# Loading the kept pieces of h for the second ConvGLU phase through SyncE's queue instead of GpSimd's

## The chip, the core and the metric

The kernel runs on one core of a Trainium2 chip. The metric is the device time of one execution, in microseconds (us). Times are given for three runs of the kernel before, and one further execution was taken with the profiler.

The engines are called as the profile calls them: PE is TensorE, DVE is VectorE, ACT is ScalarE, POOL is GpSimd, SP is SyncE. Each works through its own list of instructions in order, and a DMA is an instruction in the list of the engine that issues it.

## What is computed

The reference is a decoder trunk of two layers. After the attention part, each layer does this (cut to what matters):

```python
h = h + mix
h = h + conv_glu(rmsnorm(h, ffn_norm[i]), ffn_w_in[i], ffn_conv_w[i], ffn_conv_b[i], ffn_w_out[i])
...
def conv_glu(hn, w_in, conv_w, conv_b, w_out):
    u, gate_in = jnp.split(hn @ w_in, 2, axis=-1)
    c = (conv_w[0] * shift_right(gate_in, 2) + conv_w[1] * shift_right(gate_in, 1)
         + conv_w[2] * gate_in + conv_b)
    return (jax.nn.gelu(c, approximate=False) * u) @ w_out
```

h is 1024 positions by 1024 features, the middle of the gated part 2816 wide, all in float32. The change lies in the last line: the product with `w_out`, and the residual h that is added to it.

## The kernel before

Float32 products are made of three matmuls: weights and data are each split into a rounded high half (a cast on ACT, line 202) and the rest, the low half (a subtraction on DVE or POOL, line 203); `mm3` multiplies high by high, high by low and low by high (line 228).

Both products of the ConvGLU use Strassen's scheme in Winograd's form: seven block products in place of eight, on sums of blocks. The first phase (`ffn_in`) makes the gated values, adds them up to the seven operands, and writes these to DRAM as the tiles `md` (seven products by eleven pieces of 128x512). It also needs the room that h took, so h has been written to DRAM earlier (`hs`, line 564).

The second phase, `ffn_out`, is run once per layer. It goes through its seven products in order (`jobs`, n = 0 to 6). Each has eleven pieces; a piece is a load of `md` into a `wraw` tile (line 763, three buffers, issued by SP), its two halves `mh` (ACT) and `ml` (DVE), the two halves `whi` (ACT) and `wlo` of a weight block `a`, and twelve matmuls (four output tiles by three). For n = 0 and 1 the low weight half is made on POOL, from n = 2 on DVE. The weight blocks of n = 3 to 6 are sums of the loaded ones, which POOL makes in place (line 742, 44 additions of 128x512 per layer); `a10` is wanted by product 3, `a00` by 4, `a11` by 2 and then, changed, by 5, `a01` by 6.

The output tiles are added on DVE (`add`, line 734) into a new h. Where a quarter of h is first complete but for the residual, `kept` loads the old piece of h from `hs` into a tile `kept` of three buffers and adds it: 16 pieces a layer, four after product 3 (for q = 0 to 3 in the low half of the positions), four after product 4 and eight after product 5. The load is issued by POOL.

A scheduler sets the order of the instructions on each engine from estimated times; a load stands where its buffer is expected to come free. So the first three `kept` loads stand early, and the fourth stands behind the first addition of a kept piece, whose buffer it takes over.

Of the kernel before, what the change touches and what calls it, by code (L numbers as in the profile page):

```python
# [122 lines left out]
class Trunk:  # L123
# [596 lines left out]
    def ffn_out(self, ctx, h, hs, layer, md, first):  # L720


        nc, tc, t = self.nc, self.tc, self.t
        wp, pm = self.wp, self.pm
        Q, N = KD // 2, NFT // 2
        lo, hi = slice(0, BW), slice(BW, S)
        kp = Lines(ctx.enter_context(tc.tile_pool(reuse_waits="tile", name="kept", bufs=3)))
        ap = Lines(ctx.enter_context(tc.tile_pool(reuse_waits="tile", name="wout", bufs=1)))

        a = [[[None] * 2 for m in range(2)] for i in range(N)]  # L730
        late = [(1, 0, i) for i in range(N)]
        for m, k, i in late[:5] + [(m, k, i) for m, k in ((0, 0), (0, 1), (1, 1)) for i in range(N)] + late[5:]:
            a[i][m][k] = ap.tile([P, Q, P], F32, name=f"a{m}{k}_{i}")
        add = lambda out, x, y: nc.vector.tensor_tensor(out=out, in0=x, in1=y, op=OP.add)

        def load(m, k, i):
            nc.sync.dma_start(out=a[i][m][k], in_=t["ffn_w_out"][layer, i, k, m])

        def sums(out, one, two, op):
            def at(i):  # L740
                out_, x, y = [a[i][m][k] for m, k in (out, one, two)]
                nc.gpsimd.tensor_tensor(out=out_, in0=x, in1=y, op=op)  # L742
                return out_
            return at


        plain = lambda m, k: lambda i: a[i][m][k]
        jobs = [(plain(0, 0), (0, 1)), (plain(0, 1), (1, 1)), (plain(1, 1), (1, 0)), (sums((1, 0), (1, 0), (1, 1), OP.add), None),
                (sums((0, 0), (1, 0), (0, 0), OP.subtract), None), (sums((1, 1), (1, 1), (0, 0), OP.subtract), None),
                (sums((0, 1), (0, 1), (0, 0), OP.subtract), None)]  # L750
        for i in list(range(len(first), N)) + list(range(len(first))):
            load(0, 0, i)

        def kept(f, bs):
            x = kp.tile([P, BW], F32, name="kept")
            nc.gpsimd.dma_start(out=x, in_=hs[:, f, bs])
            add(h[:, f, bs], h[:, f, bs], x)

        for n, (weight, ahead) in enumerate(jobs):
            ps = [pm.tile([P, BW], F32, name="mm") for q in range(Q)]  # L760
            for i in range(N):
                raw = wp.tile([P, BW], F32, name="wraw", bufs=self.wbufs[0])
                nc.sync.dma_start(out=raw, in_=md[n][i])
                if ahead:
                    load(*ahead, i)
                xh, xl = [self.block_tile(j, R) for j in range(2)]
                self.split(xh, xl, raw, eng=nc.vector)
                if n == 0 and i < len(first):
                    wh, wl = first[i]
                else:  # L770
                    wh, wl = [wp.tile([P, Q, P], R, name="w" + x, bufs=self.wbufs[1]) for x in ("hi", "lo")]
                    self.split(wh, wl, weight(i), eng=nc.vector if n > 1 else nc.gpsimd)
                for q in range(Q):
                    self.mm3(ps[q], [((wh[:, q], wl[:, q]), (xh, xl))], first=i == 0, last=i == N - 1)
            for q in range(Q):
                h00, h01, h10, h11 = [h[:, 2 * q + m, bs] for m in range(2) for bs in (lo, hi)]
                if n == 0:
                    nc.scalar.copy(out=h01, in_=ps[q])
                elif n == 1:
                    add(h00, ps[q], h01)  # L780
                elif n == 2:
                    nc.scalar.copy(out=h10, in_=ps[q])
                elif n == 3:
                    nc.scalar.copy(out=h11, in_=ps[q])
                    kept(2 * q, lo)
                elif n == 4:
                    add(h01, ps[q], h01)
                    add(h10, h10, h01)
                    add(h11, h11, h01)
                    nc.vector.tensor_copy(out=h01, in_=h11)  # L790
                    kept(2 * q, hi)
                elif n == 5:
                    add(h10, ps[q], h10)
                    add(h11, ps[q], h11)
                    kept(2 * q + 1, lo)
                    kept(2 * q + 1, hi)
                else:
                    add(h01, ps[q], h01)
# [1230 lines left out]
```

## Time and profile before

| | us |
|---|---|
| median of three runs | 3007.69 |
| lowest and highest | 3003.44, 3019.6 |
| the profiled execution | 3006.23 |
| its span in the trace | 3004.5 |

| engine | busy us | share of the span |
|---|---|---|
| PE | 2835.7 | 94% |
| DVE | 2193.2 | 73% |
| ACT | 1341.1 | 45% |
| POOL | 1036.9 | 35% |

The busy times say how much of the span an engine had an instruction running; matmuls are pipelined, and their listed durations overlap, so the distance between two starts is the better measure of a matmul. `ffn_out` runs from about 1229 to 1450 us in layer 0 and from about 2620 to 2845 us in layer 1.

### The profile page before, as it was taken

How to read it: one execution, taken by the hardware profiler on the slowest of the kernel's cores; microseconds unless marked ns; L12 is line 12 of the kernel's file. 1: busy time of each engine (PE TensorE's matmuls, PEld its weight loads, DVE VectorE, ACT ScalarE, POOL GpSimd, SP SyncE). 2: the span in 40 equal slices, each digit the busy share in tenths (PEclk: the TensorE clock that was granted, in tenths of full speed). 3: DMA queues.
4: the chain of work that ended last, by engine and by line, in shares of the span. 5: the costliest groups of instructions: out<-in, count | busy, mean ns of one | idle time of the engine just before them, and what ended most of it. 6: DMA issues, size and time to landing. Idle time of an engine off the chain costs nothing. (4 is left out here: it accounts for less than half of the span.)

```text
span 3004.5 us, 40784 instructions
## 1 busy us (share of the span) xinstructions
PE 2835.7 (94%) x14278; PEld 2191.3 (73%) x14278; DVE 2193.2 (73%) x3290; ACT 1341.1 (45%) x2433; POOL 1036.9 (35%) x800
## 2 busy tenths in 40 slices
PE   8999999999899999969998899999979999996997
PEld 6776777677678888858886656566858888885886
DVE  7766657875798777566798577777489777864787
ACT  6424436663334333424644444344343333443474
POOL 4332420104434444480333500010435444384133
PEclk9999989999999999989999899999989999998998
DMA  4344565535123333733321300012113333363421
GB/s 142 111 147 127 158 199 151 156 96 172 42 99 109 106 105 106 244 97 112 102 90 58 111 18 24 12 43 102 68 51 128 105 106 103 122 234 92 123 64 57
DMA packets 238846, 322.26 MB, mean 107 GB/s; under 512 B 64465, under 2 KB 109009, under 8 KB 238641
## 3 DMA queue, kind: packets, MB, share of 16 engines
q1 hardware_dynamic: 230896, 300.79, 32.1%
q10 hardware_dynamic: 5184, 10.49, 0.9%
q0 software_dynamic: 2560, 8.39, 0.9%
q8 instruction: 112, 1.84, 0.3%
q14 instruction: 94, 0.76, 0.1%
HBM read 219.37 MB, written 99.09 MB: 106 GB/s over the span
## 5 line engine op out<-in xcount | busy, mean ns | idle before, releaser
L228 PE MATMUL mm<-x,whi 128*128 128x512 f32 x1760 | 556.0, 396 | 27.1 <-DVE x L203 14.5
L228 PE MATMUL mm<-mh,wlo 128*128 128x512 f32 x968 | 380.2, 393 | 51.9 <-DVE wlo L203 51.9
L228 PEld LDWEIGHTS mm<-x,whi 128*128 128x128 f32 x1760 | 335.2, 191 | 108.5 <-DVE x L203 22.0
L228 PE MATMUL mm<-xh,whi 128*128 128x512 f32 (+1 forms) x1016 | 405.1, 399 | 6.5 <-ACT xh L208 6.5
L228 PE MATMUL mm<-xh,wlo 128*128 128x512 f32 (+1 forms) x1016 | 397.5, 391 | 1.2 <-POOL wlo L203 1.2
L228 PE MATMUL mm<-xl,whi 128*128 128x512 f32 (+1 forms) x1016 | 390.8, 392 | 0.5 <-DVE xl L209 0.5
L228 PE MATMUL mm<-ml,whi 128*128 128x512 f32 x968 | 380.2, 393 | 1.6 <-DVE ml L203 1.4
L228 PE MATMUL mm<-mh,whi 128*128 128x512 f32 x968 | 379.8, 392 | 0.0
L203 POOL TENSOR_TENSOR wlo<-wraw,whi 128x512 fp32r<-128x512 f32 (+2 forms) x150 | 206.8, 1384 | 429.1 <-ACT whi L202 360.2
L228 PE MATMUL mm<-x,wlo 128*128 128x512 f32 x880 | 345.9, 395 | 1.1 <-DVE wlo L203 1.1
L202 ACT CAST whi<-raw 128x512 fp32r<-128x512 f32 x274 | 169.3, 619 | 323.1 <-PE mm L228 267.0
L203 POOL TENSOR_TENSOR wlo<-raw,whi 128x512 fp32r<-128x512 f32 x114 | 169.6, 1489 | 333.9 <-ACT whi L202 323.5
L228 PEld LDWEIGHTS mm<-mh,wlo 128*128 128x128 f32 x968 | 183.3, 189 | 91.6 <-DVE wlo L203 53.2
L228 PEld LDWEIGHTS mm<-xh,whi 128*128 128x128 f32 x1016 | 195.1, 192 | 50.4 <-ACT xh L208 7.2
L228 PEld LDWEIGHTS mm<-xl,whi 128*128 128x128 f32 x1016 | 194.8, 192 | 44.3 <-issue 5.1
L228 PEld LDWEIGHTS mm<-xh,wlo 128*128 128x128 f32 x1016 | 194.9, 192 | 42.2 <-POOL wlo L203 2.0
L228 PEld LDWEIGHTS mm<-ml,whi 128*128 128x128 f32 x968 | 183.2, 189 | 42.4 <-DVE ml L203 3.1
L228 PEld LDWEIGHTS mm<-mh,whi 128*128 128x128 f32 x968 | 183.6, 190 | 38.8 <-ACT mh L202 0.6
L228 PEld LDWEIGHTS mm<-x,wlo 128*128 128x128 f32 x880 | 168.5, 192 | 37.1 <-DVE wlo L203 2.6
L203 DVE TENSOR_TENSOR ml<-wraw,mh 128x512 fp32r<-128x512 f32 x154 | 134.0, 874 | 65.8 <-ACT mh L202 62.5
L1123 ACT ACTIVATE w<-s 128x512 f32<-128x512 f32 (+1 forms) x192 | 94.0, 491 | 167.1 <-PE s L1121 149.3
L202 ACT CAST whi<-a 128x512 fp32r<-128x512 f32 x148 | 91.9, 622 | 147.6 <-PE mm L228 90.3
(432 smaller groups left out, 5757.0 us busy)
## 6 DMA issues: line engine op xcount, KB each, us to landing
raw<-in_ffn_w_in SPq DMA_DIRECT2D x176, 256.0 KB
md<-u SPq DMA_DIRECT2D x154, 256.0 KB
wraw<-md SPq DMA_DIRECT2D x154, 256.0 KB
a<-in_ffn_w_out SPq DMA_DIRECT2D x88, 256.0 KB
wraw<-in_hyb_w_in SPq DMA_DIRECT2D x52, 256.0 KB
hs<-h SPq DMA_DIRECT2D x32, 256.0 KB
kept<-hs POOLq DMA_DIRECT2D x32, 256.0 KB, 3.0
wraw<-in_ple_w_gate SPq DMA_DIRECT2D x32, 256.0 KB
```

Source lines behind the costliest of these rows:

```text
L202: nc.scalar.copy(out=hi, in_=src)
L203: (eng or nc.gpsimd).tensor_tensor(out=lo, in0=src, in1=hi, op=OP.subtract)
L228: nc.tensor.matmul(ps, lhsT=w, rhs=x, start=first and i == 0, stop=last and i == len(seq) - 1)
L1123: nc.scalar.activation(out=w[:, :n], in_=s[:, :n], func=AF.Exp, scale=MLA_SCALE)
```

## The change

One line of `kept` names another engine:

```diff
         def kept(f, bs):
             x = kp.tile([P, BW], F32, name="kept")
-            nc.gpsimd.dma_start(out=x, in_=hs[:, f, bs])
+            nc.sync.dma_start(out=x, in_=hs[:, f, bs])
             add(h[:, f, bs], h[:, f, bs], x)
```

The 32 loads leave POOL's list and stand in SP's, and the scheduler places them anew. PE's list is the same in both kernels. In the rows below a name ends in the number of its buffer; layer 1 has the same pattern with other numbers.

POOL's list of the kernel before, layer 0, the last additions of weight blocks with the loads of the fourth to seventh kept piece among them:

```order
L742 TENSOR_TENSOR a01_10_11695<-a01_10_11695,a00_10_11684 128x512
L742 TENSOR_TENSOR a11_4_11700<-a11_4_11700,a00_4_11678 128x512
L742 TENSOR_TENSOR a11_5_11701<-a11_5_11701,a00_5_11679 128x512
L756 DMA kept_12765<-hs0_7126 128x512
L742 TENSOR_TENSOR a11_6_11702<-a11_6_11702,a00_6_11680 128x512
L756 DMA kept_13029<-hs0_7126 128x512
L756 DMA kept_13036<-hs0_7126 128x512
L742 TENSOR_TENSOR a11_7_11703<-a11_7_11703,a00_7_11681 128x512
L756 DMA kept_13043<-hs0_7126 128x512
L742 TENSOR_TENSOR a11_8_11704<-a11_8_11704,a00_8_11682 128x512
L742 TENSOR_TENSOR a11_9_11705<-a11_9_11705,a00_9_11683 128x512
L742 TENSOR_TENSOR a11_10_11706<-a11_10_11706,a00_10_11684 128x512
```

In the changed kernel the additions stand there alone; 39 of the 44 additions of a layer stand ahead of the fourth load before, and none stands ahead of it on SP's list.

SP's list of the changed kernel, layer 0, from the last pieces of product 2 (`md0_2`) to the first of product 3:

```order
L763 DMA wraw_12445<-md0_2_9_7825 128x512
L763 DMA wraw_12468<-md0_2_10_7826 128x512
L756 DMA kept_12765<-hs0_7126 128x512
L763 DMA wraw_12499<-md0_3_0_7827 128x512
L756 DMA kept_13029<-hs0_7126 128x512
L756 DMA kept_13036<-hs0_7126 128x512
L763 DMA wraw_12522<-md0_3_1_7828 128x512
L756 DMA kept_13043<-hs0_7126 128x512
L763 DMA wraw_12545<-md0_3_2_7829 128x512
```

Before, the `md` loads stood there one after the other; now the fourth kept load goes out between the last load of product 2 and the first of product 3. On DVE the order of this stretch is unchanged:

```order
L734 TENSOR_TENSOR h2_0_11659<-h2_0_11659,kept_12753 128x512
L203 TENSOR_TENSOR wlo_12384<-a11_6_11702,whi_12383 128x512
L203 TENSOR_TENSOR ml_12426<-wraw_12422,mh_12425 128x512
L734 TENSOR_TENSOR h2_2_11660<-h2_2_11660,kept_12757 128x512
L734 TENSOR_TENSOR h2_4_11661<-h2_4_11661,kept_12761 128x512
L203 TENSOR_TENSOR wlo_12407<-a11_7_11703,whi_12406 128x512
L203 TENSOR_TENSOR ml_12449<-wraw_12445,mh_12448 128x512
L734 TENSOR_TENSOR h2_6_11662<-h2_6_11662,kept_12765 128x512
L203 TENSOR_TENSOR wlo_12430<-a11_8_11704,whi_12429 128x512
L203 TENSOR_TENSOR ml_12472<-wraw_12468,mh_12471 128x512
L203 TENSOR_TENSOR wlo_12453<-a11_9_11705,whi_12452 128x512
L203 TENSOR_TENSOR ml_12502<-wraw_12499,mh_12501 128x512
```

The scheduler moves the four additions of kept pieces that belong behind product 3 up into product 2; nothing of this moved with the change. `kept_12765` is the fourth piece, and the low halves of the ninth, tenth and eleventh weight block of product 2 stand behind its addition.

SP's list of the changed kernel, layer 0, at the end of product 5 (`md0_5`):

```order
L763 DMA wraw_13218<-md0_5_7_7856 128x512
L763 DMA wraw_13241<-md0_5_8_7857 128x512
L756 DMA kept_13050<-hs0_7126 128x512
L756 DMA kept_13312<-hs0_7126 128x512
L756 DMA kept_13315<-hs0_7126 128x512
L763 DMA wraw_13264<-md0_5_9_7858 128x512
L756 DMA kept_13320<-hs0_7126 128x512
L763 DMA wraw_13287<-md0_5_10_7859 128x512
```

On POOL `kept_13050` followed right behind the additions shown above; on SP it stands behind all the loads of products 3 and 4 and nine loads of product 5.

## Rows read from the trace of the kernel before

**Rows 1.** Windows of layer 0: engines' busy us (x instructions), granted clock, DMA

```profile
core 0: us, PE busy (x) PEld busy (x) DVE busy (x) ACT busy (x) POOL busy (x), PEclk, DMA share, GB/s
1313.00:1337.00 24.00, 0.07 (x1) 0.00 (x0) 1.54 (x2) 1.14 (x2) 23.41 (x21) 0.58 0.13 41
...
1341.00:1370.00 29.00, 29.00 (x130) 23.98 (x129) 19.95 (x29) 17.21 (x31) 2.32 (x2) 1.00 0.49 136
```

**Rows 2.** Who waited for whom, 1215 to 1460 us: total, times, longest

```profile
POOL kept L756 <- DVE h L734: 95.2, 9, 66.4
...
DVE h L734 <- DMA kept<-hs: 24.8, 4, 23.8
```

**Rows 3.** Timeline of PE, layer 0: start, duration, instruction, idle before it

```profile
1289.84 0.39 PE L228 MATMUL mm<-mh,whi 128*128 128x512 f32 x1
...
1308.42 0.39 PE L228 MATMUL mm<-ml,whi 128*128 128x512 f32 x1
1310.04 0.50 PE L228 MATMUL mm<-mh,wlo 128*128 128x512 f32 x1 [1.22 <-DVE wlo L203]
...
1337.66 0.79 PE L228 MATMUL mm<-mh,wlo 128*128 128x512 f32 x1 [24.59 <-DVE wlo L203]
...
1341.11 0.39 PE L228 MATMUL mm<-ml,whi 128*128 128x512 f32 x1
```

**Rows 4.** Timeline of DVE, layer 0

```profile
1299.73 1.77 DVE L734 TENSOR_TENSOR h<-h,kept 128x512 f32<-128x512 f32 x1
...
1308.22 1.76 DVE L203 TENSOR_TENSOR wlo<-a,whi 128x512 fp32r<-128x512 f32 x1
1309.91 1.77 DVE L203 TENSOR_TENSOR ml<-wraw,mh 128x512 fp32r<-128x512 f32 x1
1335.46 1.55 DVE L734 TENSOR_TENSOR h<-h,kept 128x512 f32<-128x512 f32 x1 [23.78 <-DMA kept<-hs]
1336.93 0.68 DVE L203 TENSOR_TENSOR wlo<-a,whi 128x512 fp32r<-128x512 f32 x1
```

**Rows 5.** Timeline of POOL, layer 0

```profile
1234.36 1.29 POOL L203 TENSOR_TENSOR wlo<-a,whi 128x512 fp32r<-128x512 f32 x1 [8.40 <-ACT whi L202]
...
1300.91 3.45 POOL L742 TENSOR_TENSOR a<-a,a 128x512 f32<-128x512 f32 x2
...
1332.30 0.55 POOL L756 DMA_DIRECT2D kept<-hs  x1
```

**Rows 6.** All instructions that touch the tile kept: durations in ns; from issue to landing

```profile
L756 POOL DMA_DIRECT2D kept<-hs x32: 536/536/706, 1224.2 to 2835.5; - x32
...
DMA to landing us min/median/max: 2.9/3.0/4.4
```

**Rows 7.** Timeline of DVE, layer 1

```profile
2700.13 1.77 DVE L203 TENSOR_TENSOR ml<-wraw,mh 128x512 fp32r<-128x512 f32 x1
2728.28 1.41 DVE L734 TENSOR_TENSOR h<-h,kept 128x512 f32<-128x512 f32 x1 [26.38 <-DMA kept<-hs]
...
2738.91 0.68 DVE L203 TENSOR_TENSOR wlo<-a,whi 128x512 fp32r<-128x512 f32 x1
2739.51 0.68 DVE L203 TENSOR_TENSOR ml<-wraw,mh 128x512 fp32r<-128x512 f32 x1
```

**Rows 8.** Timeline of POOL, layer 1

```profile
2701.31 23.71 POOL L742 TENSOR_TENSOR a<-a,a 128x512 f32<-128x512 f32 x19
2724.97 0.55 POOL L756 DMA_DIRECT2D kept<-hs  x1
```

**Rows 9.** Timeline of PE, layer 1

```profile
2730.34 0.80 PE L228 MATMUL mm<-mh,wlo 128*128 128x512 f32 x1 [26.11 <-DVE wlo L203]
```

**Rows 10.** Timeline of SP's queue, layer 0

```profile
1304.93 0.32 SPq L763 DMA_DIRECT2D wraw<-md  x1
```

**Rows 11.** Chain that ended last, layer 1: start, us, a load that it passes through

```profile
2657.82 3.82 DMA wraw<-md
```

**Rows 12.** A window elsewhere in the program, columns as in rows 1

```profile
1640.00:1650.00 10.00, 8.32 (x35) 6.03 (x34) 9.83 (x8) 3.51 (x6) 7.43 (x6) 1.00 0.07 20
```

## Prediction

> **What bounds the kernel now.** PE is busy for 94% of the span, so a gain can only come from its gaps. I looked for windows in which PE's busy time falls near zero beside a line that the change touches, then at who waits for whom there, then at the timelines of the engines in that chain. In layer 0 PE does nothing from 1313 to 1337 us; POOL alone is busy [rows 1]. It waits 24.59 us for a `wlo` from DVE [rows 3]; DVE waits 23.78 us for a kept load [rows 2, 4]; and that load, the fourth, is issued by POOL only at 1332.30 [rows 5], because 39 additions stand ahead of it on POOL's list. From issue to landing a kept load takes 2.9 to 4.4 us [rows 6], so the wait is nearly all queueing behind POOL's additions. The buffer had been free since 1301.50: the addition of the first kept piece starts at 1299.73 and takes 1.77 [rows 4]. Layer 1 repeats it: DVE waits 26.38, PE 26.11 [rows 7, 9], and POOL issues the load at 2724.97 [rows 8]. Afterwards PE runs without a gap [rows 1], so what is won here reaches the end.
>
> **The wait itself.** On SP the fourth load waits for its buffer (1301.50 in layer 0), and for nothing of POOL's. The next `md` load went out at 1304.93 [rows 10], so SP was idle there. The price of a landing through SP is not in the kept rows; the nearest are 3.0 for kept through POOL [rows 6] and 3.82 for an `md` load through SP [rows 11]. Either way it lands by 1305.4, and DVE reaches the addition only at 1309.91 + 1.70 = 1311.61. Cover 6.2 us: the wait goes to zero, and I take no cost for the landing.
>
> **What is late next.** POOL's additions are still to be made, and DVE no longer stands still beside them. While both work, DVE starts an operation every 1.70 us (1308.22, 1309.91 [rows 4]) where alone it starts one every 0.60 (2738.91, 2739.51 [rows 7]); POOL makes two additions in 3.45, thus also one per 1.70 [rows 5], where alone it needs 1.22 (19 in 23.71 in layer 1, the first beside DVE's last operation: 1.70 + 18 x 1.22 [rows 8]). So they take turns. A piece needs two DVE operations (`wlo`, `ml`): 3.40 us. PE needs twelve matmuls of 0.2266 (83 starts from 1289.84 to 1308.42 [rows 3]): 2.72. As long as POOL adds, PE therefore loses 0.68 us per piece. PE has no lead to cover it: it had caught up with DVE already (idle 1.22 at 1310.04 [rows 3]).
>
> How long does POOL add? In layer 0 it starts additions every 1.70 from 1300.91, so one at 1312.8; from there to 1332.30, at 1.22, are 16, and 5 follow the load on its list: 21. In layer 1 it is 18 after the first of the 19 [rows 8], plus 5: 23. At one per DVE operation, 21 give 10 pieces and 23 give 11.
>
> **The sum.**
> - Layer 0: the ninth piece's `wlo` starts after the addition, at 1313.31, and is ready 1.77 later, at 1315.08. PE started on it at 1337.66, so 22.58 us go. PE also resumed at the lower clock: the granted clock of the idle window averages 0.58 [rows 1], and eight matmul steps from 1337.66 to 1341.11 took 3.45 instead of 8 x 0.2266 = 1.81 [rows 3]: another 1.64. Won 24.2; given back 10 x 0.68 = 6.8. Net 17.4.
> - Layer 1: DVE reaches the addition at 2700.13 + 1.70 = 2701.83, `wlo` is ready at 2705.30, PE started at 2730.34 [rows 9]: 25.04, and I take the same 1.64. Won 26.7, given back 11 x 0.68 = 7.5. Net 19.2.
> - Together 36.6 us. The profiled execution took 3006.23, so 2969.6; the median of the runs is 1.5 above it, 3007.69, so **2971**.
>
> The Trainium skill (SBUF — State Buffer, section "SBUF: two separate sides") says that DVE and GpSimd share one port pair as an exclusive lock and that the loser blocks for the whole instruction. The trace agrees in kind, but a pair takes 1.70, less than the 0.60 + 1.22 = 1.82 that full blocking would give. By 1.82 a piece costs 3.64, the give-back is 21 x 0.92 = 19.3 instead of 14.3, and the time is 2976; I go by the measured 1.70.
>
> **What else moves.** POOL loses 32 issues of 0.54 us [rows 6] and SP gains 32 of about 0.32 [rows 10]; neither list is full. The first three kept loads go out on SP in the rush of loads before product 0. Their cost there is bounded below by zero (POOL's next operation stood idle 8.40 us before, so it gains nothing) and above by three whole landings of 3.82 in a row: `wlo` of the fourth piece was ready at 1234.36 + 1.29 = 1235.65, and PE, counted back 26 pieces of 2.72 from 1308.8, needed it at 1238.1, which leaves 2.4 of slack, so 3 x 3.82 - 2.4 = 9 us per layer. I take zero, since three issues (1.0 us) fit in the slack; half the bound, about 4 a layer, goes into the range. The loads after products 4 and 5 wait for the same additions as before, and SP's loads behind them wait for later DVE operations still, so they delay nobody; DVE's other waits for kept pieces in this layer are 24.8 - 23.8 = 1.0 us in all [rows 2], and DVE runs pieces ahead of PE there.
>
> **Rivals.**
> - *The whole wait is won.* If DVE is not slowed by POOL's remaining additions, nothing is given back: 24.2 + 26.7 = 50.9, time 2957. Against it: every DVE operation of this form beside an addition took about 1.77 [rows 4]. 8%.
> - *No change, by the clock.* In the new stretch PE works 2.72 of every 3.40 us, after one gap of about 2 us. If the granted clock fell and stayed low, a matmul would take 0.43 and a piece 5.2 us; 10 x 2.45 and 11 x 2.45 eat 24.5 and 27.0, all of the gain: 3008. For it: the clock did fall in the long gap. Against: a window with 35 matmuls in 10 us, the pace expected here (12 per 3.40), kept a granted clock of 1.00 [rows 12]. A single short fall is made good, since PE can do 2.72 against 3.40. 6%.
> - *No change, because the queue is not what matters.* The load would still come late on SP. Against: SP issued at 1304.93 and the order puts the load ahead of that one. The Trainium skill (DMA: Bandwidth & Descriptors, section "Issuing engines are not separate DMA queues") says that DMAs of all engines run on the same 16 DMA engines and that another issuer saves only the time to initiate. By that rule alone 32 x 0.54 = 17 us leave POOL, off the path, and the time stays 3007.7; but the trace shows the time lost before the issue, in POOL's list. 4%.
> - *Slower: SP is held.* POOL spent 95.2 us per layer waiting for DVE before kept loads, 66.4 of it ahead of the first load after product 4 [rows 2]. If SP sat in that wait with `md` loads behind it, PE would run on the eight operand tiles it has (8 x 2.72 = 21.8) and then lack 66.4 - 21.8 = 44.6 per layer: 3007.7 + 89.2 - 36.6 = 3060. It decides from about eight `md` loads behind the waiting load that are wanted before its addition. Against: on SP that load stands behind nine loads of product 5, next to loads that wait for later additions. 4%.
>
> **How the numbers follow.** The forecast has 78%. The range reaches down to the whole wait won, 2957, and up to the lock's 2976 plus 4 per layer for the early loads: 2984; it leaves out the no-change and slower cases, 14%, and the tails. 0.5% (15 us) is about what a measurement of this kernel can tell from no change: the forecast and the first rival lie below, so faster 86%, same 10%, slower 4%.
>
> **What would show it.** Right: PE's gaps of 24.59 and 26.11 shrink to about 2 us; DVE's line of waits for kept falls below 2 us in each layer; DVE runs at 1.70 per operation for some 36 us afterwards, with PE waits of about 0.7 per piece for `wlo`, and the granted clock at 1.00; POOL's additions end about 1348 instead of 1344. Wrong: a gap of over 5 us on PE in this stretch, a fall of the clock that lasts, SP waiting in front of `md` loads that ACT then waits for, or a new gap of PE in product 0.

## The result and the profile after

| | before | after |
|---|---|---|
| median of four runs each | 3008.19 us | 2971.39 us |
| lowest to highest | 3003.44 to 3019.6 | 2971.08 to 2971.57 |
| ratio, 95% interval | | 0.9871 [0.9855, 0.9887] |
| profiled execution | 3006.23 | 2971.57 |
| span in the trace | 3004.5 | 2969.1 |

The change is faster by 37 us, where a median of 2971 was forecast. The four runs of the kernel before take in the three shown ahead.

The windows of layer 0 after, columns as in [rows 1]:

```profile
core 0: us, PE busy (x) PEld busy (x) DVE busy (x) ACT busy (x) POOL busy (x), PEclk, DMA share, GB/s
1220.00:1240.00 20.00, 20.00 (x90) 16.53 (x89) 14.99 (x23) 7.34 (x14) 5.21 (x5) 1.00 0.81 261
1313.00:1337.00 24.00, 20.85 (x84) 14.97 (x83) 24.00 (x16) 9.84 (x18) 24.00 (x15) 1.00 0.29 82
```

From 1313 to 1337 us, where PE had made one matmul [rows 1], it now makes 84, at a granted clock of 1.00, PE's full clock. At 0.2266 each, 84 are still only 19 of the 24 us. The other two engines of the chain, DVE and POOL, are busy for all of the 24 us. The waits from 1215 to 1460 us say who is late now:

```profile
PEld mm L228 <- DVE wlo L203: 10.1, 12, 1.4
PE mm L228 <- DVE wlo L203: 5.0, 12, 0.9
...
DVE h L734 <- DMA kept<-hs: 0.2, 1, 0.2
```

DVE's 24.8 us before kept loads [rows 2] have become 0.2, and one PE gap of 24.59 [rows 3] has become twelve of up to 0.9, all for `wlo`. POOL's line of waits before kept loads (95.2) is gone with its loads. The three timelines of layer 0, PE first:

```profile
1314.75 0.50 PE L228 MATMUL mm<-mh,wlo 128*128 128x512 f32 x1 [0.94 <-DVE wlo L203]
1318.15 0.50 PE L228 MATMUL mm<-mh,wlo 128*128 128x512 f32 x1 [0.38 <-DVE wlo L203]
...
1352.12 0.50 PE L228 MATMUL mm<-mh,wlo 128*128 128x512 f32 x1 [0.34 <-DVE wlo L203]
```

```profile
1311.23 1.78 DVE L734 TENSOR_TENSOR h<-h,kept 128x512 f32<-128x512 f32 x1
1312.93 1.77 DVE L203 TENSOR_TENSOR wlo<-a,whi 128x512 fp32r<-128x512 f32 x1
1314.61 1.78 DVE L203 TENSOR_TENSOR ml<-wraw,mh 128x512 fp32r<-128x512 f32 x1
...
1350.29 1.78 DVE L203 TENSOR_TENSOR wlo<-a,whi 128x512 fp32r<-128x512 f32 x1
1351.99 0.68 DVE L203 TENSOR_TENSOR ml<-wraw,mh 128x512 fp32r<-128x512 f32 x1
```

```profile
1283.83 67.68 POOL L742 TENSOR_TENSOR a<-a,a 128x512 f32<-128x512 f32 x40
```

DVE adds the fourth piece at 1311.23 with no wait ahead of it, then starts an operation every 1.70 us until 1350.29. POOL's additions run in one row to 1283.83 + 67.68 = 1351.51, 1.69 each. In the same moment DVE's operations fall to 0.68, and PE waits no more. In between, PE starts a piece every 3.40 us (1314.75, 1318.15) instead of every 2.72. Layer 1 shows the same: twelve waits of PE for `wlo`, the first of 1.99 us and the others of 0.36 to 0.39. SP's queue shows where the load went out:

```profile
1301.13 0.32 SPq L756 DMA_DIRECT2D kept<-hs  x1
1304.54 0.32 SPq L763 DMA_DIRECT2D wraw<-md  x1
```

It stood at 1332.30 on POOL [rows 5].

**Two measures for one layer.** Runs of one kernel differ by 10 us and more, and part of what two profiled executions differ by lies ahead of layer 0's `ffn_out`: ACT's first copy of product 0's result starts between 1255.0 and 1269.2 us in the executions below. So the experiments are compared by stretches of their own. The first goes from that copy (line 778) to the start of the last DVE addition that follows product 6 (line 734). The rows of layer 0, with the first and the last start, before:

```profile
L778 ACT COPY h<-mm x4: 589/597/610, 1257.4 to 1259.9; 128x512 f32<-128x512 f32 x4
...
L734 DVE TENSOR_TENSOR h<-mm,h x16: 675/684/689, 1405.4 to 1470.7; 128x512 f32<-128x512 f32 x16
```

and after:

```profile
L778 ACT COPY h<-mm x4: 590/597/611, 1259.7 to 1262.2; 128x512 f32<-128x512 f32 x4
...
L734 DVE TENSOR_TENSOR h<-mm,h x16: 675/684/689, 1388.5 to 1452.5; 128x512 f32<-128x512 f32 x16
```

1470.7 - 1257.4 = 213.3 us before, 1452.5 - 1259.7 = 192.8 after. The end of this stretch is a mark of DVE's, and a later last addition of DVE's is not always a loss to PE. So a second stretch is taken on PE alone, from the start of the last matmul of product 0 to that of product 6, 792 matmuls later. These are the two rows of layer 0 before:

```profile
1259.01 0.39 PE L228 MATMUL mm<-mh,wlo 128*128 128x512 f32 x1
...
1466.48 0.39 PE L228 MATMUL mm<-mh,wlo 128*128 128x512 f32 x1
```

and after:

```profile
1261.29 0.39 PE L228 MATMUL mm<-mh,wlo 128*128 128x512 f32 x1
...
1449.52 0.39 PE L228 MATMUL mm<-mh,wlo 128*128 128x512 f32 x1
```

1466.48 - 1259.01 = 207.5 us before, 1449.52 - 1261.29 = 188.2 after; 792 matmuls at 0.2266 would be 179.5. (Before, product 6 thus ends at about 1467 us in layer 0, and in the same way at about 2859 us in layer 1, later than the 1450 and 2845 that are given ahead.) DVE's last addition starts 4.2 us behind PE's last matmul before and 2.9 behind it after, so the first measure makes the gain of layer 0 1.3 us too large. For every kernel (line 778 is 780 where an edit shifts it; each stretch is of one profiled execution):

| kernel | to DVE's last addition, layer 0 | layer 1 | PE alone, layer 0 | layer 1 | median us | ratio to before [interval] |
|---|---|---|---|---|---|---|
| before | 213.3 | 213.3 | 207.5 | 207.4 | 3008 to 3011 | |
| after | 192.8 | 194.4 | 188.2 | 189.3 | 2971.39 | 0.9871 [0.9855, 0.9887] |
| after_again | 194.0 | 194.5 | 189.4 | 188.7 | 2966.78 | 0.9856 [0.9834, 0.9879] |
| e1_four_bufs_on_pool | 194.4 | 193.6 | 189.9 | 188.7 | 2976.49 | 0.9875 [0.9856, 0.9893] |
| e3_layer1_only | 213.2 | 194.2 | 207.6 | 189.8 | 2989.21 | 0.992 [0.9905, 0.9935] |
| e4_first_four_on_sp | 197.3 | 198.6 | 190.1 | 193.0 | 2978.2 | 0.9892 [0.9869, 0.9915] |
| e5_last_twelve_on_sp | 211.8 | 212.8 | 207.2 | 206.6 | 3007.86 | 0.9985 [0.9972, 0.9999] |
| e8_before_no_a01 | 202.0 | 200.8 | 195.0 | 195.3 | 2983.82 | 0.9902 [0.9864, 0.9939] |
| e6_after_no_a01 | 189.9 | 189.7 | 184.9 | 184.1 | 2959.69 | 0.9823 [0.9786, 0.986] |
| e7_after_no_a01_a11 | 185.7 | 187.1 | 181.1 | 181.0 | 2959.9 | 0.9804 [0.9759, 0.9849] |
| v3_sums_spread | 205.5 | 207.9 | 191.5 | 196.1 | 2990.14 | 0.9922 [0.9894, 0.9951] |
| v4_sums_spread_two | 202.4 | 196.8 | 186.7 | 181.6 | 2978.99 | 0.9887 [0.9869, 0.9906] |
| v5_into_freed_tiles | 186.0 | 185.8 | 181.8 | 181.2 | 2956.45 | 0.9816 [0.979, 0.9843] |
| v6_last_into_freed | 189.0 | 189.7 | 184.5 | 184.9 | 2962.92 | 0.9835 [0.9812, 0.9859] |

### The profile page after: what moved, and what is told of

Same layout as the page of the kernel before. It is cut to its first block, busy times and chain, and to the rows that moved or that the text cites. A ratio compares the mean times of both kernels' runs of the same rounds, so it can differ in the third digit from the quotient of the medians.

```text
span 2969.1 us, 40738 instructions
## 1 busy us (share of the span) xinstructions
PE 2842.9 (96%) x14278; PEld 2191.1 (74%) x14278; DVE 2236.3 (75%) x3290; ACT 1340.8 (45%) x2433; POOL 1035.8 (35%) x768
## 4 chain that ended last, share of the span: by engine, by line
PE 77%; DVE 12%; issue 5%; ACT 2%; DMA 2%; POOL 1%; SPq 0%; DVEq 0%; ACTq 0%; POOLq 0%
PE mm L228 57%; PE o L1106 3%; DVE ml L203 2%; PE s L1117 2%; PE s L1120 1%; PE o L1854 1%; PE tr L1842 1%; PE mm L1077 1%; PE s L1121 1%; PE z L1826 1%; DMA wraw<-md 1%; PE z L1823 1%; PE pk L1534 1%; DVE wlo L203 1%; DVE x L203 1%
## 5 line engine op out<-in xcount | busy, mean ns | idle before, releaser
L203 DVE TENSOR_TENSOR ml<-wraw,mh 128x512 fp32r<-128x512 f32 x154 | 157.1, 1025 | 65.4 <-ACT mh L202 62.6
L202 ACT CAST mh<-wraw 128x512 fp32r<-128x512 f32 x154 | 95.2, 621 | 131.7 <-DMA wraw<-md 120.2
```

Source lines behind the costliest of these rows:

```text
L202: nc.scalar.copy(out=hi, in_=src)
L203: (eng or nc.gpsimd).tensor_tensor(out=lo, in0=src, in1=hi, op=OP.subtract)
```

## The experiments

The theory is that the fourth load was late by its place in POOL's list, behind the additions, and that with this load on time DVE and POOL take turns, which gives part of the gain back. Its rivals are that POOL's DMA queue itself was late, that the gain has another source, and that the pace of 3.40 us is not POOL's doing. Where sums are left out below, the products use unsummed weights, so these kernels compute other values; they are there for their times alone.

**Place or queue.** The kernel before gets one more buffer for the kept pieces and keeps its queue (here and below, ... stands for code that is left out):

```diff
-... name="kept", bufs=3 ...
+... name="kept", bufs=4 ...
```

> The kernel before with four buffers for the kept pieces instead of three; all loads stay on GpSimd's software queue. The fourth load then needs no buffer back and stands ahead of the 39 additions on POOL's list. Place theory (the time was lost in POOL's list, behind the additions): the gaps of 24.59 and 26.11 us on PE go as they did on SyncE's queue, DVE's waits for kept fall below 3 us in all, and the time is that of the change, 2971 +- 5. Queue theory (something in the software queue itself, its landing or its descriptors, was late): the gaps stay and the time is 3008 +- 5.

The ratio is that of the change, without any kept load on SP (the median, 2976.49, lies half a microsecond above the expected range, beside 3010.82 for before in the same hour). POOL's timeline of layer 0 shows why:

```profile
1224.99 2.31 POOL L756 DMA_DIRECT2D kept<-hs  x4
...
1283.03 57.35 POOL L742 TENSOR_TENSOR a<-a,a 128x512 f32<-128x512 f32 x34
```

Four loads go out ahead of the additions, and DVE has no wait for kept pieces left. So the place in the list made the load late, and not the queue.

**Which layer.** The change is made in layer 1 alone; against the kernel before:

```diff
-            nc.gpsimd.dma_start(...
+            (nc.sync if layer else nc.gpsimd).dma_start(...
```

> The change made in layer 1 alone; layer 0 loads its kept pieces through GpSimd as before. If each layer's gap is won by itself with the shares that the prediction worked out (17.4 and 19.2), 3008.2 - 19.2 = 2989 +- 3, with the gap of about 24.6 us of layer 0 on PE still there and that of layer 1 gone. Rival (gain not additive, layer 0's is only moved to a later stage or comes from another part of the program): within 5 us of 2971 or of 3008.

The median is 2989.21, as expected. Layer 0 stays at 213.2 us and layer 1 goes to 194.2, so each layer's gain is made in that layer.

**Which loads.** `kept` is given the engine that issues its load. First the four loads after product 3 alone go out on SP; the eight after product 5 stay on POOL like the four after product 4, which are shown:

```diff
-    kept(2 * q, lo)
+    kept(2 * q, lo, nc.sync)
...
-    kept(2 * q, hi)
+    kept(2 * q, hi, nc.gpsimd)
```

> Only the four kept loads after product 3 (one of them the fourth load of the prediction... the one that comes first behind the 39 additions) go through SyncE; the twelve after products 4 and 5 stay with GpSimd. One-load theory: all of the gain hangs on that load, 2971 +- 3. Rival (the twelve later loads matter too, through POOL's waits or SyncE's place): between, 2976 to 3000.

Then the complement, with the loads after products 4 and 5 on SP:

```diff
-    kept(2 * q, lo)
+    kept(2 * q, lo, nc.gpsimd)
...
-    kept(2 * q, hi)
+    kept(2 * q, hi, nc.sync)
```

> The complement: the twelve kept loads after products 4 and 5 go through SyncE, the four after product 3 stay with GpSimd, so that the fourth still stands behind the additions. One-load theory: nothing is won, 3008 +- 5, and both gaps on PE stay within 2 us of 24.59 and 26.11. Rival (the relief of POOL by 24 issues and 66 us of waits matters): under 3000.

The complement wins next to nothing (0.9985), and its wait is the old one, on DVE and on POOL:

```profile
1334.98 0.69 DVE L734 TENSOR_TENSOR h<-h,kept 128x512 f32<-128x512 f32 x1 [24.85 <-DMA kept<-hs]
```

```profile
1331.97 0.55 POOL L756 DMA_DIRECT2D kept<-hs  x1
```

The four loads, of which only the fourth was late, win most of the gain. The expected 2971 +- 3 was missed by 4 us, and 2978.2 lies in the range that the rival had. The totals alone can't part this kernel from the changed one, since its interval reaches down to 0.9869. PE alone wins 17.4 and 14.4 us, against 19.3 and 18.1 in the changed kernel and 18.1 and 18.7 in its repeat: layer 0 is within a microsecond of the repeat, and what is missing lies in layer 1. There it has a place. DVE (the first row in layer 0, the second in layer 1), then POOL and PE in layer 1:

```profile
1344.83 3.09 DVE L203 TENSOR_TENSOR wlo<-a,whi 128x512 fp32r<-128x512 f32 x1
...
2722.29 6.67 DVE L203 TENSOR_TENSOR ml<-wraw,mh 128x512 fp32r<-128x512 f32 x1
```

```profile
2721.76 1.09 POOL L756 DMA_DIRECT2D kept<-hs  x2
2722.87 1.30 POOL L742 TENSOR_TENSOR a<-a,a 128x512 f32<-128x512 f32 x1
2724.11 0.55 POOL L756 DMA_DIRECT2D kept<-hs  x1
2724.68 3.72 POOL L742 TENSOR_TENSOR a<-a,a 128x512 f32<-128x512 f32 x3
```

```profile
2729.62 0.80 PE L228 MATMUL mm<-mh,wlo 128*128 128x512 f32 x1 [4.16 <-DVE wlo L203]
```

A DVE operation that takes 0.68 alone and 1.77 in turn took 6.67 while POOL issued loads and went on adding at 1.24 each (3.72 for three); PE then stood for 4.16. In layer 0 one took 3.09, and PE stood for 1.69. In `ffn_out` no DVE operation of lines 203 and 734 took over 1.91 in any other kernel here. By the other measure layer 0 falls 4.5 us behind the changed kernel, but 2.7 of that lie behind PE's last matmul. DVE waited there for a kept piece of product 5 (2.7 us over layer 0, in three waits), and its last additions came later:

```profile
1432.86 0.69 DVE L734 TENSOR_TENSOR h<-h,kept 128x512 f32<-128x512 f32 x1 [1.87 <-DMA kept<-hs]
```

So in this one profiled execution the loads that stayed on POOL's list cost something too, mostly by what happened to DVE beside their issue.

**The price of the additions ahead of the load.** This is the kernel before without the sums for product 6:

```diff
-(sums((0, 1), (0, 1), (0, 0), OP.subtract), None)]
+(plain(0, 1), None)]
```

> The kernel before, kept loads on GpSimd, with the eleven sums for product 6 left out (the product uses the unsummed weights, so its values are others): 28 instead of 39 additions ahead of the fourth load. Place theory: the load is issued 11 x 1.22 = 13.4 us earlier in each layer, PE's gaps fall from 24.59 and 26.11 to about 11 and 13, and the time is 3008 - 27 = 2981 +- 4. Queue theory (the additions are not what the load waits for): 3008 +- 5.

Its waits in layer 0:

```profile
DVE h L734 <- DMA kept<-hs: 14.2, 4, 11.7
...
PE mm L228 <- DVE wlo L203: 12.8, 2, 12.5
```

PE's gap is 12.5 us in both layers, 12.1 and 13.6 less than before (13.4 expected), and the layers are shorter by 11.3 and 12.5. The wait shrinks with the list ahead of the load.

**Does POOL's work take part of the gain back?** The same edit was made on the changed kernel, and then the sums for product 5 were left out too (`plain(1, 1)`):

> The changed kernel with the eleven sums for product 6 left out (values of product 6 are others): 33 instead of 44 additions on POOL per layer. Theory of turns (each addition lets DVE pass once in 1.70 us, and PE loses 0.68 us per piece while POOL adds): POOL's additions end 11 x 1.70 = 19 us earlier, 5.5 of the 12 pieces no longer lose 0.68, 3.7 us per layer: 2971 - 7.5 = 2964 +- 2, with 6 to 7 waits of PE for wlo per layer instead of 12. Rival (the pace of 3.40 comes from DVE's or ACT's own work behind the kept pieces, not from POOL): 2971 +- 2, with 12 waits.

> The changed kernel with the sums for products 5 and 6 left out, 22 per layer (values of both products are others). Theory of turns: POOL's additions end about when the fourth kept piece is added, nothing is given back: 2971 - 12 x 0.68 x 2 = 2955 +- 3, at most one wait of PE for wlo of over 0.1 us in each layer there. Rival: 2971 +- 2.

The waits from 1215 to 1460 us of the first, and the only wait of PE for `wlo` from 1300 to 1365 us in the second:

```profile
PE mm L228 <- DVE wlo L203: 3.5, 6, 1.6
```

```profile
1321.35 0.50 PE L228 MATMUL mm<-mh,wlo 128*128 128x512 f32 x1 [1.27 <-DVE wlo L203]
```

PE has twelve waits in the changed kernel, six without eleven of the sums and one without 22, as the theory of turns has it; the rival would have kept twelve. Without the eleven sums the layers are 2.9 and 4.7 us shorter (3.7 expected), without the 22, 7.1 and 7.3 (12 x 0.68 = 8.2 expected); on PE alone these are 3.4 and 5.3, and 7.1 and 8.3. In the totals 2959.69 lies below the expected 2964 +- 2 and 2959.9 above 2955 +- 3. Totals of so few runs can't place the two against each other: in the profiled executions alone the second kernel reached the end of product 0 7.3 us later (1265.9 to 1258.6). The stretches can.

**Versions to beat both.** Here the sums for products 5 and 6 go into a buffer of their own, which holds them back:

```diff
+                if apart:
+                    out_ = kp.tile([P, Q, P], F32, name="wsum", bufs=1)
                 nc.gpsimd.tensor_tensor(out=out_, in0=x, in1=y, op=op)
...
-... (sums((1, 1), (1, 1), (0, 0), OP.subtract), None),
-                (sums((0, 1), (0, 1), (0, 0), OP.subtract), None)]
+... (sums((1, 1), (1, 1), (0, 0), OP.subtract, True), None),
+                (sums((0, 1), (0, 1), (0, 0), OP.subtract, True), None)]
```

> A version meant to beat both: the changed kernel with the sums for products 5 and 6 written by GpSimd into one buffer of their own instead of in place, so that they can't run ahead and come one per piece in those products. Theory of turns: only 23 additions are left ahead of and in the stretch, which wins the 8 us per layer that were given back, as long as DVE in products 5 and 6 (one operation of 0.60 and one beside an addition, 1.70: 2.30) and the chain addition, ACT's cast, DVE's rest on one buffer stay below PE's 2.72 per piece: 2956 +- 3. Rival (the chain on one buffer takes over 2.72, for example 1.7 + 0.7 + 0.6 = 3.0 per piece): 22 x 0.3 = 6.6 per layer given back there, 2969 +- 4.

It lost to the changed kernel, by more than its rival had (2990.14 against 2969 +- 4): 13 us a layer to DVE's last addition, 3.3 and 6.8 of them on PE within products 1 to 6. Additions of product 5 on POOL:

```profile
1407.99 1.67 POOL L744 TENSOR_TENSOR wsum<-a,a 128x512 f32<-128x512 f32 x1 [1.46 <-DVE wlo L203]
1411.11 1.29 POOL L744 TENSOR_TENSOR wsum<-a,a 128x512 f32<-128x512 f32 x1 [1.46 <-DVE wlo L203]
1413.86 1.67 POOL L744 TENSOR_TENSOR wsum<-a,a 128x512 f32<-128x512 f32 x1 [1.46 <-DVE wlo L203]
```

Each waits 1.46 for the piece before to go through cast and rest: 3.12 and 2.75 a piece, over PE's 2.72. With two such buffers, and two for kept:

```diff
-... name="kept", bufs=3 ...
+... name="kept", bufs=2 ...
...
-... name="wsum", bufs=1)
+... name="wsum", bufs=2)
```

> As the version with the sums for products 5 and 6 in a buffer of their own, but with two such buffers (and two instead of three for the kept pieces, for the room). If the 3.1 us per piece of the one-buffer version came from POOL waiting for DVE's rest of the piece before (addition 1.3 to 1.7, cast 0.62, rest 0.69, in one chain), two buffers let the addition run beside cast and rest; the longest of them is 1.7, below PE's 2.72, and products 4 to 6 take again 91 to 95 us per layer, while products 1 to 3 stay at 92: 7 us per layer less than the changed kernel, 2957 +- 3. Rival (the slow pace is DVE's, beside POOL's additions, or the third kept load comes late on two buffers): 2965 or more.

The total is better, but still 12 us behind the changed kernel in its repeat. The chain on one buffer was thus a part only. Up to the end of product 6 PE is not behind at all: 186.7 and 181.6 us, where the changed kernel takes 188.2 and 189.3. It loses right behind, where the changed kernel has no wait of PE:

```profile
1447.35 0.39 PE L228 MATMUL mm<-mh,wlo 128*128 128x512 f32 x1
...
1450.37 0.50 PE L228 MATMUL mm<-ph,wlo 128*128 128x512 f32 x1 [2.19 <-POOL wlo L203]
...
1459.88 0.47 PE L228 MATMUL mm<-ph,whi 128*128 128x512 f32 x1 [2.63 <-DVE h L734]
```

The first row is the last matmul of product 6 in layer 0, the other two belong to the next stage. Layer 1 has the same two waits, of 1.61 and 4.10 us. Additions in products 5 and 6 thus delay the stage behind, which needs POOL and DVE for its own operands. Over that stage's first 32 matmuls PE loses 7.0 and 7.8 us against the kernel before; beside the two waits, the granted clock of layer 0 is 0.89 from 1447.5 to 1463 us. What became of the rest was not followed.

The changed kernel was timed beside it:

> The changed kernel once more, on the chip and in the hour of the version above, for the comparison of the two and for the spread of its stages: 0.9871 of the kernel before within its interval (2971 where that takes 3008 to 3011), products 1 to 3 at 102 +- 1 us in each layer and products 4 to 6 at 91 +- 1. Rival (the 4.6 and 3.5 us that products 4 to 6 took less than before were chance): 94 to 96 there.

It repeats: 194.0 and 194.5 us. (The expectation splits the stretch at ACT's copy behind product 3. The parts are 103.1 and 90.9 us in layer 0 and 102.2 and 92.3 in layer 1, but that copy is a poor mark: 15 matmuls more of PE's list lie ahead of it than before in layer 0, and 14 in layer 1. So the 4.6 and 3.5 us that products 4 to 6 seemed to win are mostly the mark's, and the table uses the whole stretch.)

The last two place the sums where DVE has room, with no buffer: over weight tiles that are done with. Those for product 5 go into the tiles of product 3, those for product 6 into those of product 4:

```diff
-(sums((1, 1), (1, 1), (0, 0), OP.subtract), None),
-(sums((0, 1), (0, 1), (0, 0), OP.subtract), None)]
+(sums((1, 0), (1, 1), (0, 0), OP.subtract), None),
+(sums((0, 0), (0, 1), (0, 0), OP.subtract), None)]
```

> The changed kernel with one more edit: GpSimd's sums for product 5 are written over the tiles that product 3 has used, those for product 6 over the tiles that product 4 has used, so that they can't run before those products' weights are split, and come one per piece in products 3 and 4, not in 5 and 6. Theory of turns: 22 additions are left ahead, they end about when the fourth kept piece is added, and one addition per piece leaves DVE at 0.60 + 1.70 = 2.30 against PE's 2.72, so products 1 to 3 take about 92 instead of 102 us per layer; products 5 and 6 keep the additions out, so that the stage behind them loses nothing, and products 4 to 6 take 91 to 95: 3 to 10 per layer less, 2957 +- 6, ratio 0.983. Rival (the additions cost the same wherever they run, as the two versions with a buffer of their own suggest): 2970 or more.

and the second line alone:

> The same for the sums of product 6 alone: 33 additions run ahead as they come, 11 during product 4. Theory of turns: as in the run that left out the eleven sums, about 6 of the 12 waits of PE for wlo are left in each layer, 3.8 us per layer less than the changed kernel: 2963 +- 4, between it and the version above. Rival: 2970 or more.

The medians are 2956.45 and 2962.92, where 2957 and 2963 were expected. The first has the stretches of the kernel that left 22 sums out (181.8 and 181.2 us on PE, beside 181.1 and 181.0) and leaves nothing out; PE waits for `wlo` once a layer, and six times in the second. Its interval ends at 0.9843. Those of the changed kernel begin at 0.9855 and, in the repeat, at 0.9834, so the totals part it from the first only; the stretches part it from both. POOL and DVE of layer 0:

```profile
1333.36 1.68 POOL L742 TENSOR_TENSOR a<-a,a 128x512 f32<-128x512 f32 x1 [0.63 <-DVE wlo L203]
1335.67 1.68 POOL L742 TENSOR_TENSOR a<-a,a 128x512 f32<-128x512 f32 x1 [0.63 <-DVE wlo L203]
```

```profile
1333.21 0.68 DVE L203 TENSOR_TENSOR ml<-wraw,mh 128x512 fp32r<-128x512 f32 x1
1333.81 1.78 DVE L203 TENSOR_TENSOR wlo<-a,whi 128x512 fp32r<-128x512 f32 x1
1335.51 0.68 DVE L203 TENSOR_TENSOR ml<-wraw,mh 128x512 fp32r<-128x512 f32 x1
```

There is one addition per piece, every 2.30 us: of DVE's two operations one takes 1.70, the other 0.60, together below PE's 2.72.

## Why the prediction was right

- **The wait itself**: right. The load was to go out at about 1301.5 and to be there before DVE at 1311.61; it went out at 1301.13, and DVE added at 1311.23 without a wait. That its place was the cause, and nothing of the queue, is shown by the four buffers on POOL.
- **What is late next**: right, and shown by taking POOL's work away. A DVE operation starts every 1.70 us, thus a piece every 3.40; PE's waits behind the first are 0.34 to 0.39 in the idle column and 0.68 in the pace.
- **How long POOL adds**: slightly short. 21 and 23 additions, thus 10 and 11 pieces, were forecast; it was (1351.51 - 1311.23) / 1.69 = 24 in layer 0, and PE waited for twelve pieces in both layers. The additions end at 1351.5 in layer 0, not at 1348, since POOL's last row of them began later and with one more to make, 40 at 1283.83 where it had been 39 at 1282.62:

```profile
1282.62 49.73 POOL L742 TENSOR_TENSOR a<-a,a 128x512 f32<-128x512 f32 x34
```

- **The sum**: right in its parts. PE's list is the same in both kernels, so a matmul's start after can be set against the same matmul's start before. In layer 0 the lead is largest, 24.4 us, at the first piece behind the old gap (24.2 forecast); at product 6's last matmul 17.0 are left (1466.48 to 1449.52), so 7.5 went back in eleven slow pieces (6.8 in ten forecast, the term that was mis-sized), and 17.4 were forecast to stay. PE had ended product 0 2.3 us later in this execution, and the ninth piece was ready no later for it, so that the layer by itself wins 19.3. In layer 1 the lead is 25.6 at its largest (26.7) and 7.5 went back (7.5), so it wins 18.1 (19.2). The repeat wins 18.1 and 18.7. Against the kernel without the 22 sums, 7.1 and 8.3 went back. The lead at the end is the 35.4 us by which the trace's span fell: 17.0, 18.1, and 0.3 between the layers, against 36.6 forecast.
- **The microsecond**: that the median was hit to one is luck. The repeat's median is 2966.78, and runs of the kernel before lie 16 us apart.
- **The lock**: by the Trainium skill's rule (SBUF — State Buffer, section "SBUF: two separate sides") the loser blocks for the whole instruction, which by the estimate in the prediction would give 1.82 for a pair and 2976. The trace shows DVE and POOL going one by one, for 23 operations in a row, but at 1.70 a pair.
- **The early loads**: taken at zero, rightly. From 492 to 1308 us PE is 2.2 to 2.3 us later than before throughout, and no more so at product 0's end than ahead of `ffn_out`, so the early loads cost PE nothing. In layer 1 its lead stays at 17.3 us from 2357 us to the gap, so there they cost nothing either.
- **The rivals**: the whole wait is won only where POOL has nothing to add, as the kernel without 22 sums shows. The clock stayed at 1.00 in the stretch. SP was not held: in the trace after, its longest wait ahead of a kept load in layer 0 is 6.7 us, where POOL's was 66.4, and ACT's longest wait for an `md` load there fell from 25.5 to 5.6.

## What to carry to other kernels

A DMA is issued where it stands in its engine's list. So look first at what stands ahead of it there, and only then at how long the transfer takes; an earlier place on the old engine (here by one more buffer) can do as much as another engine. When a wait goes, ask what the waiting engine will share with its neighbour: here DVE's free run became a run in turn with GpSimd, and 7 to 8 us of 26 a layer went back. Work that is early without need can be held back without another buffer by letting it write over something that is free only later; where it then runs decides whether that pays.

## What the runs showed of the hardware

- In layer 0 of the changed kernel, DVE's two-input operations and GpSimd's additions of 128x512 alternate one to one over 39 us: 1.70 us per pair, against 0.60 and 1.22 alone.
- Beside a GpSimd that issues loads between its additions the alternation can break, as the DVE operations of 3.09 and 6.67 us above show. Other issues did not do it: beside four loads from 1340 to 1344 us in the kernel with four buffers no DVE operation took over 1.91. What decides is open. The Trainium skill (SBUF — State Buffer, section "SBUF: two separate sides") tells of the reverse, a DVE operation in a two-port mode that holds up a load issued by GpSimd; no run here shows that one.
- Two gaps of PE of equal length were followed by different clocks. After one of 2.03 us, which ended at 1316.10, the kernel with four loads on SP ran at a mean granted clock of 0.88 over the next 14 us:

```profile
1316.00:1330.00 14.00, 13.40 (x49) 10.30 (x50) 14.00 (x10) 3.98 (x8) 14.00 (x9) 0.88 0.27 73
```

49 matmuls stand where 59 of 0.2266 would fill the 13.40 us. PE next waited for a `wlo` at 1329.68, four pieces of 3.40 after 1316.10, so the fall cost nothing while DVE set the pace, as the prediction had it. In the fastest version a gap of 2.03 us ended at 1324.90, and the clock is 1.00 from 1313 to 1348 us.
